# Short-rowed tiles in a pool of their own: every fp32r operand at a multiple of 256 bytes

## The chip, the cores and the metric

The kernel runs on one core of a Trainium2 chip. The metric is the time of one execution in microseconds (us), as the device counts it; times are compared as medians of several executions. The kernel before takes 1206.37 us (three runs, 1205.99 to 1206.79). A difference of about 0.2%, some 2.4 us, is the least that such a measurement tells from none.

## The reference

Two layers of a hybrid decoder trunk over 512 tokens of width 1024. Cut to what matters here:

```python
def hybrid_layer(x, c_silu, cos, sin, norm_g, w_ada, b_ada, w_in, sinks, w_br_a, w_br_b, w_br_c, w_out):
    mod = c_silu @ w_ada + b_ada
    shift, scale, gate = jnp.split(mod, 3, axis=-1)
    u = rms_norm(x, norm_g) * (1 + scale[:, None]) + shift[:, None]
    z = u @ w_in                     # (512 x 1024) @ (1024 x 8772)
    (aq, ak, av, ag, iq, ik, iw, bq, bk, bv, bg, cq, ck, cv, cg, ma, mb, mc) = jnp.split(z, SPLIT_OFFSETS, axis=-1)
    ya = dsa_attention(...)          # top-128 keys by an indexer, softmax
    yb = swa_sinks_attention(...)    # window of 128 keys, softmax with sinks
    yc = stick_breaking_attention(...)
    merged = (jax.nn.sigmoid(ma) * ((ya * silu(ag)) @ w_br_a)
              + jax.nn.sigmoid(mb) * ((yb * silu(bg)) @ w_br_b)
              + jax.nn.sigmoid(mc) * ((yc * silu(cg)) @ w_br_c))
    return x + gate[:, None] * (merged @ w_out)
```

All inputs and outputs are float32. The large products (u @ w_in, the three branch products, merged @ w_out) are most of the arithmetic.

## The kernel before

**Products in three parts.** TensorE multiplies float32 in a reduced form (fp32r) in one pass. To keep float32's accuracy, each operand of a large product is split into a high part and the rest: the weights into `whi` and `wlo`, the activations into `uh0` to `uh7` and `ul0` to `ul7` (one pair for each 128 features of u). A product is then the sum of three: hi by hi, hi by rest, rest by hi (`ttile`, and in the same way `branch_item` and `out_phase`). The gated mixer outputs, split, stand in `Y`; merged, split, stands in `vc` and `va` (high) and in `Q` and `KH` (rest).

**Tiling.** All activations lie transposed: 128 features on the partitions, the 512 tokens along the row. A tile of z is 128 columns by 512 tokens and is summed over eight blocks of 128 features, so it takes 24 products of a 128x128 block of weights (held in the array) with a 128x512 block of activations (streamed through it). A weight tile (`wstage`, then `whi` and `wlo`) holds four blocks of weights side by side, 512 floats or 2,048 bytes in a row; four such tiles of each are in use by turns. In the phase that makes the values (`v_phase`) it is the other way round: a block of `uh` is held and 364 columns of `whi` are streamed.

**Order.** The program is recorded first (`Recorder`), and a planner with a table of costs gives each instruction an engine and a place (`forward`, `order`); `emit` then writes each engine's instructions in that order. Nothing of this looks at where a tile lies in SBUF. The planner also picks the slot of a rotating tile (which of the four `whi`, which of the fourteen `t`).

**Where tiles lie.** Each partition of SBUF has one row of bytes. A pool lays its tiles one after another, in the order in which each is first asked for, each rounded up to a multiple of 32 bytes. Tiles of a fixed name come from the pool `const` (`fixed`, L589 and 590), the rotating ones from the pool `sb` (`Places.make`, L237 and 238), as the order of `emit` first reaches them (`Place.real`, L221 to 224). Rows of 2,048 or 4,096 bytes thus stand among rows of 4, 8, 16, 32, 64, 96 and 896 bytes, and each of those shifts all that follow it.

In the built program the tiles come to lie so, in bytes from the start of a partition, and by how much they exceed a multiple of 256:

| tile | first address before | over a multiple of 256 |
|---|---|---|
| `vc`, `va`, `Y` (five), `wstage` (four) | 36288, 44480, 52672, 60864 | 192 |
| `whi`, `wlo`: two slots of each | 93664, 97760 and 95712, 103904 | 224 |
| `whi`, `wlo`: the other two of each | 116224, 120320 and 118272, 124416 | 0 |
| `uh0`, `ul0` | 101856, 110048 | 224 |
| `uh1` to `uh7`, `ul1` to `ul7` | 122368 to 155136 | 0 |
| `Q` (both), `KI`, first `KH` | 185856, 183808, 177664 | 0 |
| second `KH` | 198848 | 192 |
| `klow0`, `klow1` | 22400, 25472 | 128 |
| `xm2` to `xm7` | 213376 to 223616 | 128 |

The blocks that a product takes out of a tile start at multiples of 256 bytes within it, so these numbers hold for the operands too. Of the program's fp32r products with a stream of 512 columns and all 128 rows there are 3,708:

| streamed operand | held operand | products |
|---|---|---|
| at a multiple of 256 | at a multiple of 256 | 1,333 |
| at a multiple of 256 | 224 over | 1,245 |
| 192 or 224 over | at a multiple of 256 | 536 |
| 192 or 224 over | 224 over | 594 |

The remaining fp32r products have streams of 128, 256, 364 or 384 columns, or take only half of the rows (the `pairs` of the low parts).

Of the kernel before, what the change touches and what calls it, by code (L numbers as in the profile page):

```python
# [25 lines left out]
F32 = mybir.dt.float32  # L26
F32R = mybir.dt.float32r
BF16 = mybir.dt.bfloat16
# [5 lines left out]
P = 128  # L34
# [116 lines left out]
         "m8": 2, "mx": 2, "nm": 2, "den": 2, "wstage": 4, "whi": 4, "wlo": 4, "ps_z": 3, "ps_s": 5}  # L151


class View:


# [73 lines left out]
class Places:  # L230
# [4 lines left out]
        self.tiles = []  # L235

    def make(self, shape, dtype, slot):  # L237
        return self.pool.tile(list(shape), dtype, name=self.name, tag=f"{self.name}_{slot}", bufs=1)


class Instr:
# [336 lines left out]
@with_exitstack  # L578
def trunk(ctx, tc, xT, vecs, w_ss, w_gt, w_first, w_t, w_v, w_br, w_o, rope, consts, out):
    nc = tc.nc  # L580
    const = ctx.enter_context(tc.tile_pool(name="const", bufs=1))
    sb = ctx.enter_context(tc.tile_pool(name="sb", bufs=1))
    ps = ctx.enter_context(tc.tile_pool(name="ps", bufs=1, space=bass.MemoryType.PSUM))
# [2 lines left out]
    rec = Recorder(tc, nc, ps, sb)  # L586
    PE, ACT, DVE, POOL, SP = (rec.engine(e) for e in ("PE", "ACT", "DVE", "POOL", "SP"))

    def fixed(name, shape, dt=F32):  # L589
        return rec.fixed(const.tile(shape, dt, name=name))  # L590

    def zbank():
        return rec.tile("ps_z", [P, S])
# [17 lines left out]
    f = lambda ap: ap.bitcast(F32)  # L611
# [25 lines left out]

    ACT.preload_act_table_set("natural_log_exp_and_others")
    small = fixed("small", [P, 16 + 40 * L + P], F32)
    SP.dma_start(small, vecs)  # L640
    csb, o = small[:, 0:8], 8
# [3 lines left out]
    sink, o = small[:, o:o + 8 * L], o + 8 * L  # L645
    ident = small[:, o:o + P]
    nones = fixed("nones", [P, P], F32R)
    DVE.memset(f(nones), -1.0)
    epst = fixed("epst", [P, 1], F32)
    DVE.memset(epst, EPS)  # L650
    cs = fixed("cs", [P, 8], F32)
# [957 lines left out]
```

## Time and profile before

| what | value |
|---|---|
| median of three runs | 1206.37 us |
| the profiled execution's own time | 1205.66 us |
| its span, first to last instruction | 1203.5 us |
| mean granted TensorE clock | 0.996 |
| ScalarE (ACT) busy | 565.8 us, 47% of the span |
| GpSimd (POOL) busy | 257.3 us, 21% |
| HBM read, written | 125.39 MB, 4.19 MB |

The profile names an engine's instructions by line, operation and tiles: "ps_z<-uh,whi" writes the PSUM tile ps_z from uh and whi. Nearly every instruction has the line of `emit` (L556, or L554 for pairs), so groups are told apart by their tiles. PE is TensorE's multiplications, PEld its loads of the held operand, DVE is VectorE. The duration that a multiplication has in the profile (some 395 ns at 512 columns) covers its way through the array, in which the next one has already begun; how fast they follow one another is read from their starts.

### The profile page before, as it was taken

The numbers are of one execution on the slowest core, as the hardware profiler recorded it, in microseconds if no ns is written. First come the engines' busy times: TensorE is split into PE (matmuls) and PEld (weight loads), VectorE is DVE, ScalarE is ACT, GpSimd is POOL, SyncE is SP. The second block draws the span as 40 slices with busy tenths as digits, with TensorE's granted clock in tenths as the row PEclk, the third lists the DMA queues.
The fourth block names the chain that finished last, engine by engine and source line by source line (L and its number), as shares of the span: only waits on it lengthen the run. The fifth ranks groups of instructions, "written<-read, shape, count | busy, mean of one in ns | idle before, by whom it ended". The sixth has DMA issues, their size and how long they took to land.

```text
span 1203.5 us, 17819 instructions
## 1 busy us (share of the span) xinstructions
PE 1181.2 (98%) x6006; PEld 969.7 (81%) x6006; DVE 958.3 (80%) x2094; ACT 565.8 (47%) x1177; POOL 257.3 (21%) x291
## 2 busy tenths in 40 slices
PE   9999999999999999999999999999999999999997
PEld 8799777788887887778898987777878778877886
DVE  6867999999888878786486699989897888667754
ACT  6533677564456532642143167665544654234222
POOL 1100355442010111001201016453221010111120
PEclk9999999999999999999999999999999999999999
DMA  9644323243434444344533433323342324323343
GB/s 318 229 121 123 91 71 89 87 123 114 122 100 129 132 141 140 88 129 148 165 112 98 136 95 81 86 71 115 115 123 79 97 80 123 96 66 84 94 123 99
DMA packets 81914, 139.39 MB, mean 116 GB/s; under 512 B 10016, under 2 KB 22560, under 8 KB 81824
## 3 DMA queue, kind: packets, MB, share of 16 engines
q1 hardware_dynamic: 80672, 136.17, 38.8%
q10 hardware_dynamic: 1152, 2.10, 0.5%
q8 instruction: 47, 0.77, 0.3%
q14 instruction: 43, 0.35, 0.1%
HBM read 125.39 MB, written 4.19 MB: 108 GB/s over the span
## 4 chain that ended last, share of the span: by engine, by line
PE 86%; DVE 6%; DMA 3%; ACT 2%; SPq 2%; issue 1%; POOL 0%; DVEq 0%; ACTq 0%
PE ps_z L556 67%; PE ps_s L556 14%; PE ps_s L554 5%; DMA wstage<-in_w_first 2%; DVE t L556 2%; SPq L556 2%; ACT t L556 1%; DVE KH L556 1%; DMA m<-zs 1%; DVE m L556 0%; DVE Y L556 0%; DVE zc L556 0%; DVE Q L556 0%; DVE wlo L556 0%; DMA wstage<-in_w_ss 0%
## 5 line engine op out<-in xcount | busy, mean ns | idle before, releaser
L556 PE MATMUL ps_z<-uh,whi 128*128 128x512 f32 (+1 forms) x908 | 360.1, 398 | 2.8 <-ACT e L556 1.2
L556 PE MATMUL ps_z<-uh,wlo 128*128 128x512 f32 (+1 forms) x908 | 357.0, 394 | 0.0
L556 PE MATMUL ps_z<-ul,whi 128*128 128x512 f32 (+1 forms) x908 | 356.0, 392 | 0.0
L556 POOL TENSOR_TENSOR wlo<-wstage,whi 128x512 fp32r<-128x512 f32 (+1 forms) x131 | 172.6, 1318 | 623.3 <-DVE whi L556 302.1
L556 PEld LDWEIGHTS ps_z<-uh,whi 128*128 128x128 f32 x908 | 170.6, 188 | 41.6 <-issue 2.1
L556 PEld LDWEIGHTS ps_z<-uh,wlo 128*128 128x128 f32 x908 | 171.0, 188 | 38.2 <-issue 1.7
L556 PEld LDWEIGHTS ps_z<-ul,whi 128*128 128x128 f32 x908 | 171.1, 188 | 34.6
L556 DVE TENSOR_TENSOR wlo<-wstage,whi 128x512 fp32r<-128x512 f32 (+2 forms) x241 | 159.0, 663 | 14.3 <-ACT whi L556 4.9
L556 ACT CAST whi<-wstage 128x512 fp32r<-128x512 f32 (+2 forms) x149 | 88.5, 597 | 169.1 <-PE ps_z L556 128.6
L556 DVE CAST whi<-wstage 128x512 fp32r<-128x512 f32 (+2 forms) x171 | 71.0, 416 | 112.9 <-PE ps_z L556 96.2
L556 PE MATMUL ps_z<-Y,whi 128*128 128x512 f32 x384 | 121.1, 396 | 1.1 <-ACT e L556 1.1
L556 ACT ACTIVATE e<-ps_z 128x512 f32<-128x512 f32 x68 | 40.3, 594 | 133.3 <-PE ps_z L556 133.0
L556 PEld LDWEIGHTS ps_z<-Y,whi 128*128 128x128 f32 x384 | 71.7, 188 | 18.3 <-issue 1.4
L556 ACT ACTIVATE e<-e 128x512 f32<-128x512 f32 x96 | 60.4, 631 | 37.3 <-DVE e L556 36.2
L556 ACT ACTIVATE t<-t 128x512 f32<-128x512 f32 x120 | 71.3, 627 | 13.2 <-DVE t L556 8.9
L556 POOL CAST whi<-wstage 128x512 fp32r<-128x512 f32 (+2 forms) x52 | 33.8, 651 | 200.8 <-PE ps_z L556 135.2
L556 PE MATMUL ps_z<-Y,wlo 128*128 128x512 f32 x192 | 75.7, 395 | 0.0
L556 ACT ACTIVATE t<-t,nm 128x256 f32<-128x256 f32 (+3 forms) x128 | 65.1, 510 | 17.3 <-DVE nm L556 17.1
L556 PE MATMUL ps_s<-small,t 128*128 128x128 f32 x432 | 59.1, 275 | 4.7 <-DVE t L556 4.4
L556 PEld LDWEIGHTS ps_s<-small,t 128*128 128x128 f32 x432 | 51.1, 142 | 14.2 <-issue 5.8
L556 DVE MAX8 m<-score 128x8 f32<-128x256 f32 (+2 forms) x96 | 53.5, 557 | 1.9
L556 PE MATMUL ps_s<-KH,Q 128*128 128x256 f32 (+3 forms) x280 | 52.0, 309 | 1.4 <-DVE t L556 1.4
(210 smaller groups left out, 2028.5 us busy)
## 6 DMA issues: line engine op xcount, KB each, us to landing
wstage<-in_w_t SPq DMA_DIRECT2D x212, 256.0 KB, 2.8
wstage<-in_w_v SPq DMA_DIRECT2D x48, 182.0 KB, 2.4
Y<-in_w_ss SPq DMA_DIRECT2D x16, 512.0 KB, 6.9
m<-zs SPq DMA_DIRECT2D x128, 64.0 KB, 2.0
wstage<-in_w_gt SPq DMA_DIRECT2D x32, 256.0 KB, 2.7
wstage<-in_w_ss SPq DMA_DIRECT2D x32, 256.0 KB, 2.8
wstage<-in_w_o SPq DMA_DIRECT2D x32, 256.0 KB, 2.8
wstage<-in_w_first SPq DMA_DIRECT2D x16, 256.0 KB, 4.0
```

The costliest lines, as they stand in the source:

```text
L554: self.real[engine].matmul(*[real(a) for a in q[:3]], start=q[3], stop=True, skip_group_check=True)
L556: getattr(self.real[engine], y.op)(*[real(a) for a in y.args], **{k: real(v) for k, v in y.kw.items()})
```

## The change

A function `pool_for` sends each tile whose row in bytes is no multiple of 256 to a new pool, `tiny`, that is laid out ahead of all others; it is used for the fixed tiles and for the rotating ones. One more tile, `gap` (128 bytes, never read or written), goes to that pool, so that it takes 1,920 bytes and ends at 18432, a multiple of 256. `const` and `sb` then begin at, and hold nothing but, multiples of 256.

```diff
+LINE = 256
+tiny = [None]
+
+
+def pool_for(pool, shape, dtype):
+
+    return pool if int(np.prod(shape[1:])) * (2 if dtype == BF16 else 4) % LINE == 0 else tiny[0]
+
...
     def make(self, shape, dtype, slot):
-        return self.pool.tile(list(shape), dtype, name=self.name, tag=f"{self.name}_{slot}", bufs=1)
+        return pool_for(self.pool, shape, dtype).tile(list(shape), dtype, name=self.name, tag=f"{self.name}_{slot}", bufs=1)
...
 def trunk(ctx, tc, xT, vecs, w_ss, w_gt, w_first, w_t, w_v, w_br, w_o, rope, consts, out):
     nc = tc.nc
+    tiny[0] = ctx.enter_context(tc.tile_pool(name="tiny", bufs=1))
     const = ctx.enter_context(tc.tile_pool(name="const", bufs=1))
...
     def fixed(name, shape, dt=F32):
-        return rec.fixed(const.tile(shape, dt, name=name))
+        return rec.fixed(pool_for(const, shape, dt).tile(shape, dt, name=name))
...
     DVE.memset(f(nones), -1.0)
+    fixed("gap", [P, 32], F32)
     epst = fixed("epst", [P, 1], F32)
```

No instruction is added, removed or moved: in the built program each engine's instructions stand in the order of before, with the same operands, the same slots and the same waits. Only addresses differ. Every tile of the first table lies at a multiple of 256 bytes, and so do all operands of all 5,028 fp32r products; `Y` starts at 53248, the `whi` at 94208, 98304, 116736 and 120832, `uh0` at 102400, `uh1` at 122880. In `tiny` lie the vectors of one to 24 floats, `small` and the 32-byte scratch of the top-k and the softmaxes. `small`, at 16512, has not moved. The last tile ends 128 bytes further on than before.

## Prediction

> **What bounds the kernel now.** First the page's head, its row by slices for the clock, and the chain of waits.
>
> ```profile
> span 1203.5 us, 17819 instructions
> PE 1181.2 (98%) x6006; PEld 969.7 (81%) x6006; DVE 958.3 (80%) x2094; ACT 565.8 (47%) x1177; POOL 257.3 (21%) x291
> PEclk9999999999999999999999999999999999999999
> PE 86%; DVE 6%; DMA 3%; ACT 2%; SPq 2%; issue 1%; POOL 0%; DVEq 0%; ACTq 0%
> PE ps_z L556 67%; PE ps_s L556 14%; PE ps_s L554 5%; DMA wstage<-in_w_first 2%; DVE t L556 2%; SPq L556 2%; ACT t L556 1%; DVE KH L556 1%; DMA m<-zs 1%; DVE m L556 0%; DVE Y L556 0%; DVE zc L556 0%; DVE Q L556 0%; DVE wlo L556 0%; DMA wstage<-in_w_ss 0%
> ```
>
> TensorE multiplies during 98% of the span at its full clock, and of the chain that ended last 86% is TensorE, 67% of the span in ps_z alone. So the kernel is as fast as its products follow one another. Next, what these products are: the groups of instructions with their shapes kept apart.
>
> ```profile
> L556 PE MATMUL ps_z<-uh,whi 128*128 128x512 f32 x884 | 353.3, 401 | 2.7 <-ACT e L556 1.2 <-DVE xm L556 0.9 <-ACT uh L556 0.7
> L556 PE MATMUL ps_z<-uh,wlo 128*128 128x512 f32 x884 | 350.0, 396 | 0.0
> L556 PE MATMUL ps_z<-ul,whi 128*128 128x512 f32 x884 | 349.4, 395 | 0.0
> L556 PE MATMUL ps_z<-Y,whi 128*128 128x512 f32 x384 | 121.1, 396 | 1.1 <-ACT e L556 1.1
> L556 PE MATMUL ps_z<-Y,wlo 128*128 128x512 f32 x192 | 75.7, 395 | 0.0
> ...
> L556 PE MATMUL ps_z<-Q,whi 128*128 128x512 f32 x48 | 19.0, 397 | 0.0
> ```
>
> With the five other groups of 48 (streams from vc, va and KH), 3,516 products of 512 columns go to ps_z; 192 more go to ps_s, 3,708 in all. Their durations overlap, so what counts is the step from one start to the next. The kernel before already contains both kinds of operands, and one engine runs them within microseconds of each other. The timeline of PE, start and duration in us:
>
> ```profile
> 408.08 0.39 PE L556 MATMUL ps_z<-uh,whi 128*128 128x512 f32 x1
> ...
> 410.12 0.39 PE L556 MATMUL ps_z<-uh,whi 128*128 128x512 f32 x1
> ...
> 410.80 0.39 PE L556 MATMUL ps_z<-uh,whi 128*128 128x512 f32 x1
> ...
> 412.85 0.39 PE L556 MATMUL ps_z<-uh,whi 128*128 128x512 f32 x1
> ...
> 413.55 0.39 PE L556 MATMUL ps_z<-uh,whi 128*128 128x512 f32 x1
> ...
> 418.44 0.40 PE L556 MATMUL ps_z<-uh,whi 128*128 128x512 f32 x1
> ...
> 419.14 0.40 PE L556 MATMUL ps_z<-uh,whi 128*128 128x512 f32 x1
> ...
> 423.91 0.63 PE L556 MATMUL ps_z<-Y,whi 128*128 128x512 f32 x2
> ...
> 432.22 0.63 PE L556 MATMUL ps_z<-Y,whi 128*128 128x512 f32 x2
> ...
> 435.02 0.39 PE L556 MATMUL ps_z<-uh,whi 128*128 128x512 f32 x1
> ```
>
> The addresses of the built program say what each stretch is. From 408.08 to 412.85 come 21 products, the blocks 1 to 7 of one tile of z, streams and held weights all at multiples of 256: 4.77 us, **227.1 ns a step**. From 413.55 to 418.44 come 21 again, the same streams, but from weight slots 224 over: 4.89 us, **232.9 ns**. From 419.14 to 423.91, with aligned slots, it is 4.77 us once more. From 432.22 to 435.02, 12 products stream Y, 192 over, with aligned weights: 2.80 us, **233.3 ns**. Same engine, shape and clock; only the addresses differ, and one unaligned operand of either kind is enough.
>
> **The change, part by part.** Products of 512 columns: 2,375 of the 3,708 have an unaligned operand (1,245 + 536 + 594, from the program), and all of them become aligned. A step falls from 233.0 to 227.1 ns, between 232.9 − 227.1 = 5.8 and 233.3 − 227.1 = 6.2; I take 6.0. 2,375 × 6.0 ns = **14.3 us** less of TensorE. Starts are shown to 0.01 us, 0.5 to 0.8 ns in such a step, so the bounds are 5.3 and 6.7 ns, 12.6 and 15.9 us.
>
> [...]
>
> Shorter products: the value phase streams 364 columns.
>
> ```profile
> 81.41 0.33 PE L556 MATMUL ps_s<-whi,uh 128*128 128x364 f32 x1
> ...
> 85.41 0.33 PE L556 MATMUL ps_s<-whi,uh 128*128 128x364 f32 x1
> ...
> 89.41 0.33 PE L556 MATMUL ps_s<-whi,uh 128*128 128x364 f32 x1
> ```
>
> 24 products from aligned slots of whi and wlo (81.41 to 85.41) take 4.00 us, and 24 from slots 224 over (85.41 to 89.41) take 4.00 us, 166.7 ns each. So I count nothing for the 576 of these, and nothing for the other short shapes; the bound above is 6 ns for each of the 1,320 fp32r products outside the 3,708, 7.9 us, far from this row and therefore a rival.
>
> The other engines: four casts and six subtractions of the weight split on DVE, over both kinds of slots, in one stretch:
>
> ```profile
> L556 DVE TENSOR_TENSOR wlo<-wstage,whi x6: 679/691/693, 405.8 to 422.5; 128x512 fp32r<-128x512 f32 x6
> L556 DVE CAST whi<-wstage x4: 420/424/427, 409.9 to 418.9; 128x512 fp32r<-128x512 f32 x4
> ```
>
> Minimum, median and maximum lie within 14 ns, without a second kind. DVE, and ACT and POOL by likeness, get 0. Loads: those into wstage (192 over) and those into G (a multiple of 256 today) stand at
>
> ```profile
> wstage<-in_w_o SPq DMA_DIRECT2D x32, 256.0 KB, 2.8
> G<-xsave SPq DMA_DIRECT2D x8, 256.0 KB, 2.7
> ```
>
> 0.1 us of 2.8 is 4%. The chain holds 3% DMA, 36 us, mostly at the start: at most 1.3 us gained, and 0 taken. The pool `tiny` gathers scratch of DVE, ACT and POOL in 1.9 KB; no row shows such neighbours disturbing each other, and I take 0 between −0.5 and +0.5 us.
>
> How much reaches the end: ps_z on the chain is 67% of 1203.5, 806 us. The 3,516 products at the mean step of (2,375 × 233.0 + 1,333 × 227.1) ÷ 3,708 = 230.9 ns are 812 us, and ps_z has some 55 us of shorter ones, so 806 ÷ 867 = 93% of them lie on the chain. 14.3 × 0.93 = **13.3 us**. The rest runs while TensorE waits anyway, mostly for DVE:
>
> ```profile
> PE ps_s L556 <- DVE t L556: 5.8, 4, 3.0
> PE ps_z L556 <- ACT e L556: 2.3, 2, 1.2
> ```
>
> Then what is late next. DVE is the engine closest behind: the sum of the windows 150 to 300 and 700 to 900 us, and the tightest of them (columns: window, length, busy time and instructions of PE, PEld, DVE, ACT, POOL, clock, DMA):
>
> ```profile
> 200.00:250.00 50.00, 48.29 (x250) 37.44 (x250) 47.99 (x103) 33.02 (x70) 25.32 (x28) 1.00 0.32 96
> ...
> sum 350.00, PE 344.81 PEld 273.24 DVE 326.60 ACT 212.47 POOL 147.10; mean PE 49.26 PEld 39.03 DVE 46.66 ACT 30.35 POOL 21.01
> ```
>
> DVE is busy 93% of these 350 us (stick-breaking, top-k and rotary work beside the products). They are 29% of the span and, at an even density, hold 14.3 × 0.29 = 4.1 us of the gain. DVE's 23.4 us of idle time would allow all of it, but its order is fixed and TensorE waits for it there, so some turns into longer waits: between 0 and 4.1 us; I take a third, 1.4, nearer to 0 since DVE still has over five times that idle. 13.3 − 1.4 = **11.9 us**. From the profiled execution's 1205.66 that is 1193.8; the median of before lies 0.7 us higher, at 1206.37, which gives 1194.5. I forecast **1194 us**, 1.0% less. Ends: 15.9 us all on the chain gives 1190.5, 12.6 × 0.8 − 4.1 = 6.0 us gives 1200.4.
>
> **The rivals.**
>
> 1. *DVE becomes the bound.* If TensorE's waits for DVE absorb all of the gain in the dense stretches and half of it elsewhere, 13.3 − 4.1 − 4.6 = 4.6 us stay: about 1202 us. For it: 93% busy, and waits for its t that are there already. Against: outside these windows DVE has idle time, and 86% of the chain is TensorE.
> 2. *The change does nothing.* If the step depends on something that goes along with the address (which slot was loaded when, say), or TensorE has no address term: 1206 us. For it: the 364-column rows show none. Against: the same 6 ns with Y and aligned weights, and within one tile of z. [...]
> 3. *Slower: operands meet in the same place.* Afterwards streams, held weights and the split's outputs nearly all start at multiples of 2,048 bytes. If reads that begin at equal places disturb each other by as much as misalignment costs now, the 1,333 aligned products get 6 ns longer and the others stay: +8.0 us, 1214 us. It decides if equal offsets cost more than nothing; today's rows are against it, since from 410.12 to 410.80 (0.68 us, 3 products, 227 ns) stream and held block of uh4 and whi lie exactly 18,432 bytes, nine times 2,048, apart. Only three-way meetings are untried.
> 4. *More than forecast.* If the short products gain too, up to 7.9 us, or the loads' 1.3 us, the time is 1185 to 1190 us.
>
> **How the numbers follow.** The forecast case (1190.5 to 1200.4) has 0.76: both steps of its main term are measured in this trace. Rival 1 has 0.10, rival 2 0.06, rival 3 0.04, rival 4 0.04. The range 1190 to 1201 holds the forecast case and the near end of rival 1, about 8 in 10. Faster by over 0.2% (about what a measurement of this kernel can tell from no change) are the forecast and rivals 1 and 4, 0.90; within it rival 2, 0.06; slower rival 3, 0.04.
>
> **What would show it.** In the profile after, the uh products of every tile of z should step at 227 ns, those from Y too, and none of the stretches at 233 should be left; the 364-column steps should stay at 166.7. PE's busy time should fall by about as much as the span, and its waits for DVE grow by 1 to 3 us. If steps are 227 and the span has fallen by less than 6 us, the conversion failed (rival 1), to be seen in the waits and in windows 150 to 300. If steps of 233 or more remain in the same number, it is rival 2 or 3.

## The result, and the profile after

The changed kernel takes **1194.02 us** (median of four runs, 1190.49 to 1195.28), the kernel before beside it on the same chip 1206.18 (four runs, 1205.76 to 1206.79). The ratio is 0.9894, with a 95% interval of 0.9872 to 0.9916: 1.1% faster, where 1194 was forecast. The profiled execution took 1194.35 us. Beside the later runs the kernel before spread from 1201.48 to 1207.32 us, and medians of it from 1204.72 to 1206.18, so a few runs tell less than the 0.2% that was set out above.

The head of the page and the chain of waits, after:

```profile
span 1192.2 us, 17819 instructions
PE 1167.9 (98%) x6006; PEld 968.8 (81%) x6006; DVE 961.0 (81%) x2094; ACT 565.3 (47%) x1177; POOL 256.4 (22%) x291
PE 85%; DVE 8%; ACT 2%; DMA 2%; SPq 2%; issue 1%; DVEq 0%; POOL 0%; ACTq 0%
PE ps_z L565 65%; PE ps_s L565 15%; PE ps_s L563 5%; DVE t L565 3%; SPq L565 2%; ACT t L565 1%; DVE m L565 1%; DVE KH L565 1%; DMA wstage<-in_w_first 1%; DMA m<-zs 1%; DVE Q L565 0%; DVE zc L565 0%; DMA rt<-in_rope 0%; DVE wstage L565 0%; DVE score L565 0%
```

TensorE's busy time fell by 13.3 us (from 1181.2), the span by 11.3 (from 1203.5). DVE's share of the chain grew from 6% to 8%. The groups, shapes apart:

```profile
L565 PE MATMUL ps_z<-uh,whi 128*128 128x512 f32 x884 | 350.7, 398 | 2.2 <-ACT e L565 1.2 <-DVE xm L565 1.0
L565 PE MATMUL ps_z<-uh,wlo 128*128 128x512 f32 x884 | 347.3, 393 | 0.0
L565 PE MATMUL ps_z<-ul,whi 128*128 128x512 f32 x884 | 346.8, 392 | 0.6 <-DVE ul L565 0.6
L565 PE MATMUL ps_z<-Y,whi 128*128 128x512 f32 x384 | 118.8, 390 | 1.1 <-ACT e L565 1.1
```

Each is 2.3 to 2.7 us less busy than before. That understates the gain, since durations overlap (some 390 ns each, starts 227 ns apart); the steps show it. The timeline of PE in the part where the prediction compared the tiles:

```profile
405.66 0.40 PE L565 MATMUL ps_z<-uh,whi 128*128 128x512 f32 x1
...
421.32 0.62 PE L565 MATMUL ps_z<-Y,whi 128*128 128x512 f32 x2
...
424.04 0.39 PE L565 MATMUL ps_z<-uh,whi 128*128 128x512 f32 x1
```

69 products of uh and ul take 15.66 us, 227.0 ns a step, through all four slots of the weights; the 12 of Y take 2.72 us, 226.7 ns, where the kernel before needed 233.3.

The program order is the same, so the two timelines can be joined product by product. Steps over 250 ns (a wait, or half the clock, 430 ns a step) left out:

| products of 512 columns, by their addresses before | joined | fall of a step, ns | sum, us |
|---|---|---|---|
| only the held block off 256 | 1,201 | 5.5 | 6.6 |
| only the stream off | 513 | 6.0 | 3.1 |
| both off, by different amounts | 390 | 5.8 | 2.3 |
| both off by the same 224 bytes | 164 | 3.0 | 0.5 |
| both at multiples of 256 | 1,277 | 1.3 | 1.7 |
| together | 3,545 | | 14.1 |

The other shapes: steps of 364 columns did not change, those of 256 columns (520) got 1 ns *longer*, 0.7 us in all. From the first multiplication to the last the time fell by 10.96 us, so by balance all the rest, waits and the like, took 14.1 − 0.7 − 10.96 = 2.4 us more. That balance belongs to this pair of traces and not to the change: in the trace of after_again, the same changed kernel run once more (below), the products give 14.2 us, and first to last is 15.85 us shorter than in the kernel before, so there the rest took 2.3 us *less*.

PE's waits (sum, times, longest), and DVE in the dense windows (the tightest, and the sum of 150 to 300 and 700 to 900):

```profile
PE ps_s L565 <- DVE t L565: 7.1, 7, 3.1
PE ps_z L565 <- ACT e L565: 2.3, 2, 1.2
...
PE ps_s L565 <- ACT t L565: 1.5, 2, 1.4
```

```profile
200.00:250.00 50.00, 47.83 (x246) 37.30 (x246) 48.33 (x103) 32.16 (x70) 25.34 (x28) 1.00 0.34 101
...
sum 350.00, PE 343.87 PEld 274.81 DVE 328.54 ACT 210.93 POOL 146.16; mean PE 49.12 PEld 39.26 DVE 46.93 ACT 30.13 POOL 20.88
```

The wait for DVE's t grew from 5.8 to 7.1 us, and DVE is busy 2 us more of the same 350, which now hold slightly more of the program. The loads beside the products hardly moved: wstage<-in_w_o lands in 2.7 us (2.8 before).

### The profile page after: what moved, and what is told of

Same layout as the page of the kernel before. It is cut to its first block, busy times and chain, and to the rows that moved or that the text cites. A ratio compares the mean times of both kernels' runs of the same rounds, so it can differ in the third digit from the quotient of the medians.

```text
span 1192.2 us, 17819 instructions
## 1 busy us (share of the span) xinstructions
PE 1167.9 (98%) x6006; PEld 968.8 (81%) x6006; DVE 961.0 (81%) x2094; ACT 565.3 (47%) x1177; POOL 256.4 (22%) x291
## 4 chain that ended last, share of the span: by engine, by line
PE 85%; DVE 8%; ACT 2%; DMA 2%; SPq 2%; issue 1%; DVEq 0%; POOL 0%; ACTq 0%
PE ps_z L565 65%; PE ps_s L565 15%; PE ps_s L563 5%; DVE t L565 3%; SPq L565 2%; ACT t L565 1%; DVE m L565 1%; DVE KH L565 1%; DMA wstage<-in_w_first 1%; DMA m<-zs 1%; DVE Q L565 0%; DVE zc L565 0%; DMA rt<-in_rope 0%; DVE wstage L565 0%; DVE score L565 0%
## 5 line engine op out<-in xcount | busy, mean ns | idle before, releaser
L565 DVE TENSOR_TENSOR wlo<-wstage,whi 128x512 fp32r<-128x512 f32 (+2 forms) x241 | 158.0, 659 | 12.2 <-ACT whi L565 3.7
L565 ACT ACTIVATE t<-t 128x512 f32<-128x512 f32 x120 | 71.7, 628 | 12.6 <-DVE t L565 8.9
L565 DVE SCALAR_TENSOR_TENSOR wstage<-wstage,csr 128x512 f32<-128x512 f32 x64 | 49.4, 774 | 6.0 <-DMA wstage<-in_w_ss 3.2
```

Source lines behind the costliest of these rows:

```text
L565: getattr(self.real[engine], y.op)(*[real(a) for a in y.args], **{k: real(v) for k, v in y.kw.items()})
```

## The experiments

**Place or distance?** The prediction took it that each operand by itself has to begin at a multiple of 256 bytes (theory 1, place). The rival: what counts is how far apart the stream and the held block lie, modulo 256 (distance). The 198 products above with both operands 224 over (164 of them joined) already lean to it. A kernel of products alone settles it: groups of 24, each with its own pair of offsets.

```python
for i in range(count):
    a = i % 3 * 1024 + s // es      # stream, s bytes over
    b = i % 6 * 128 + w_ // es      # held block, w_ bytes over
    nc.tensor.matmul(p[:, :n], st[kind][:, b:b + 128], mv[kind][:, a:a + n], ...)
```

> The step alone: groups of 24 products that follow one another (12 for float32), streams and held blocks moved by 0 to 256 bytes each, 512 down to 128 columns, in fp32r, bf16 and float32. All of the reference's computation is left out. Theory 1 (both operands of an fp32r product must begin at a multiple of 256 bytes): 227 ns a step at 512 columns where both offsets are 0 or 256, 233 ns at all others, however small the offset, and no difference at 364 columns and below. Rival (a smaller unit, 64 or 128 bytes, is enough): 227 ns also at offsets of 64 or 128. Rival (the distance between the two operands counts, not their place): 227 ns wherever both are moved by the same amount. Rival (the address does not matter at all, it only went along with the slots): one step for all.

Its timeline of PE. A name is type (zr fp32r, zb bf16), columns (A 512, F 256), and the offsets of stream and held block (a 0, b 32, c 64, e 128, f 160, g 192, h 224, k 256 bytes); a group's time is the difference of two starts.

```profile
119.78 5.76 PE L62 MATMUL zrA_ae<-mvr,str 128*128 128x512 f32 x24
125.38 5.76 PE L62 MATMUL zrA_af<-mvr,str 128*128 128x512 f32 x24
130.99 5.67 PE L62 MATMUL zrA_ag<-mvr,str 128*128 128x512 f32 x24
136.49 5.76 PE L62 MATMUL zrA_ah<-mvr,str 128*128 128x512 f32 x24
142.09 5.61 PE L62 MATMUL zrA_ak<-mvr,str 128*128 128x512 f32 x24
147.53 5.64 PE L62 MATMUL zrA_bb<-mvr,str 128*128 128x512 f32 x24
153.01 5.64 PE L62 MATMUL zrA_cc<-mvr,str 128*128 128x512 f32 x24
...
163.96 5.64 PE L62 MATMUL zrA_ee<-mvr,str 128*128 128x512 f32 x24
169.43 5.64 PE L62 MATMUL zrA_ff<-mvr,str 128*128 128x512 f32 x24
```

Only the held block moved by 128 (ae): 5.60 us ÷ 24 = 233.3 ns. By 256 (ak): 5.44 us, 226.7 ns. *Both* moved, by 32 (bb) or by 128 (ee): 5.48 and 5.47 us, 228 ns. Both operands off 256 and yet nearly the short step: **the distance counts, and theory 1 is wrong.** What is left for the place is 1.4 ns at most (226.7 against 228). One other distance costs less than the rest: the stream 64 bytes past the held block, modulo 256 (ag, 0 against 192, is such a one: 5.50 us, 229 ns). By this rule the 198 products that lay 224 over, both of them, should have gained about 1 ns; they gained 3.0, and the difference is not explained.

256 columns of fp32r, and bf16, from the same timeline:

```profile
302.29 3.02 PE L62 MATMUL zrF_aa<-mvr,str 128*128 128x256 f32 x24
305.15 3.00 PE L62 MATMUL zrF_ba<-mvr,str 128*128 128x256 f32 x24
307.98 3.00 PE L62 MATMUL zrF_ea<-mvr,str 128*128 128x256 f32 x24
...
346.05 5.34 PE L62 MATMUL zbA_ba<-mvb,stb 128*128 128x512 bf16 x24
351.23 5.34 PE L62 MATMUL zbA_ea<-mvb,stb 128*128 128x512 bf16 x23
```

bf16 takes 5.18 us ÷ 24 = 215.8 ns at every distance that was tried (0, 32 and 128 bytes). Groups of 12 plain float32 products, two records each, take 10.30 us at every distance, 858 ns a product, where one of fp32r is a single record and steps at some 230 ns. At 256 columns of fp32r, distance 0 takes 2.86 us, 119.2 ns, and 32 bytes 2.83 us, 117.9: the order is reversed, and the kernel's 256-column steps, which got longer by 0.7 us in all, went the same way.

**The same in the kernel.** Without the tile `gap`, all 5,028 products have both operands 128 over: place off, distance 0. With `gap` three times as long, everything lies 256 further on.

```diff
-    fixed("gap", [P, 32], F32)      # no_gap
```

```diff
-    fixed("gap", [P, 32], F32)      # gap_256
+    fixed("gap", [P, 96], F32)
```

> The changed kernel without the tile gap: const and sb begin 128 bytes earlier, so all 5,028 fp32r products have both operands 128 over a multiple of 256, at the same distances from one another as in the change. Theory 1: all 3,708 steps of 512 columns cost 6 ns more, 22 us of TensorE, of which 80 to 95% reach the end: 1212 to 1215 us, slower than even the kernel before. Rival (multiples of 128 are enough) and rival (only the distance counts, or the order of the pools): 1194 us.

> The changed kernel with a gap of 384 bytes for 128: everything behind the pool tiny lies 256 bytes further on, at odd multiples of 256. Theory 1: no change, 1194 us, within 2 us. Rival (the gain comes from starts at multiples of 512 or 2,048): 1212 to 1215 us. Rival 3 of the prediction (equal places modulo 2,048 cost something): unchanged too, since all move alike.

no_gap: 1194.33 us (1194.04 to 1195.51), ratio to before 0.991 (0.9894 to 0.9927), the time of the changed kernel. gap_256: 1192.13 us (1189.46 to 1194.16), 0.9891 (0.9873 to 0.991). Its products of 512 columns sum to within 0.2 us of the changed kernel's, so it does not matter at which multiple of 256 the tiles begin. All tiles moved alike here, so this run leaves their distances open; those are tried further below. PE's timeline in no_gap:

```profile
408.20 0.39 PE L565 MATMUL ps_z<-uh,whi 128*128 128x512 f32 x1
...
421.12 0.39 PE L565 MATMUL ps_z<-uh,whi 128*128 128x512 f32 x1
```

57 products in 12.92 us are 226.7 ns a step, with not one operand at a multiple of 256. The tile `gap` does nothing; what the change does is to keep the short rows out from between the long ones.

**Distance put back.** `whi` and `wlo` alone are moved, by 128 bytes in one kernel and by 192 (a distance of 64) in the other; 3,660 products then lie that far from their streams.

```diff
-        return pool_for(self.pool, shape, dtype).tile(...)
+        pool = split[0] if self.name in ("whi", "wlo") else pool_for(self.pool, shape, dtype)
+        return pool.tile(...)
...
+    split[0] = ctx.enter_context(tc.tile_pool(name="split", bufs=1))
+    split[0].tile([P, 32], F32, name="ahead")     # weights_192: [P, 48]
+    rest = ctx.enter_context(tc.tile_pool(name="rest", bufs=1))
+    rest.tile([P, 32], F32, name="behind")        # weights_192: [P, 16]
```

> The changed kernel with whi and wlo alone moved 128 bytes on, in a pool of their own; all else stays at multiples of 256. 3,660 of the 3,708 products then have streams at 0 and held blocks at 128. Theory 2 (what counts is the distance between the stream and the held block, modulo 256): 233.5 ns a step as in the isolated groups, 23 to 24 us more TensorE, of which 80 to 95% reach the end: 1212 to 1217 us. Rival (multiples of 128 are enough, which also explains the run without the gap): 1194 us.

> As weights_128, but whi and wlo 192 bytes on, so that the stream lies 64 bytes behind a multiple of 256 from the held block. In the isolated groups this distance cost 228.7 (stream moved by 64) and 229.4 ns (held block moved by 192). Theory 2 with these steps: 2.0 to 2.7 ns for each of 3,660 products, 7 to 10 us, 80 to 95% of it at the end: 1199 to 1204 us. Rival (every distance but 0 costs the same): 1212 to 1217 us.

weights_128: 1208.0 us (ten runs, 1204.05 to 1209.99), ratio 1.0024 (1.001 to 1.0038): the whole gain is gone and a little more. weights_192: 1198.06 us (1194.48 to 1200.42), ratio 0.9938 (0.9922 to 0.9954). The two timelines of PE, weights_128 first:

```profile
407.85 0.39 PE L567 MATMUL ps_z<-uh,whi 128*128 128x512 f32 x1
...
423.19 0.40 PE L567 MATMUL ps_z<-uh,whi 128*128 128x512 f32 x1
```

```profile
404.59 0.39 PE L567 MATMUL ps_z<-uh,whi 128*128 128x512 f32 x1
...
419.70 0.39 PE L567 MATMUL ps_z<-uh,whi 128*128 128x512 f32 x1
```

66 products each: 15.34 us, 232.4 ns, and 15.11 us, 228.9 ns. Both kernels came out faster than was expected of them: the step at 128 bytes is 232.5 ns in the mean of the kernel, not 233.5, so the products take 18.2 us longer than in the changed kernel. Against the kernel before on its own chip (1204.72 and 1206.18 us) weights_128 is 3.3 us slower and the changed kernel 12.2 faster, so some 15.4 of the 18.2 us reached the end. PE's wait for t is 2.8 us in its trace, against 7.1 in the changed kernel's; that this is where the rest went was not tested.

**Which block does the stream meet?** While a block streams, the next one is being loaded (the changed kernel's loads, PEld, are busy 968.8 us of a span of 1192.2 in which PE is busy 1167.9), so "the held block" could be a product's own or the next one's. Pairs of products alternate by 128 bytes so that only one of the two pairings is at distance 0. Other groups try 464 to 504 columns.

```python
("own",  ss=(0, 128), ws=(0, 128))    # stream of product i meets its own block at 0
("next", ss=(128, 0), ws=(0, 128))    # it meets the block of product i + 1 at 0
("both", ss=(0, 0),   ws=(0, 0)),  ("none", ss=(128, 128), ws=(0, 0))
```

> The step alone once more, fp32r, 48 products a group; all of the reference's computation is left out. Groups one: stream and held block at fixed places, 0 to 2,048 bytes apart. Groups own and next: places alternate between 0 and 128 bytes over, so that a stream lies like the block that it is multiplied with (own) or like the block that is loaded while it runs, the next one (next); own_s and next_s the same with 64 bytes. Theory 2a (the stream's reads meet those of the load of the next block): 227 ns in next, 233 in own. Theory 2b (stream and its own block): 227 in own, 233 in next. Neither counts alone: both between. Groups one: 227 at 0 and at every multiple of 256, 229 at 64, 232 to 234 elsewhere; a step that differs between 256 and 2,048 would show a larger unit. Columns: 504 to 464 show between 512 (6 ns) and 448 (1 to 4 ns) how the cost of 128 bytes fades.

Its timeline of PE, groups of 48 (onen is a fixed distance of 2,048 bytes; nC is 480 columns, a at distance 0, e at 128; nD 464):

```profile
152.62 11.04 PE L60 MATMUL zonen<-mvr,str 128*128 128x512 f32 x48
163.50 11.14 PE L60 MATMUL zown<-mvr,str 128*128 128x512 f32 x48
174.48 11.20 PE L60 MATMUL znext<-mvr,str 128*128 128x512 f32 x48
185.52 11.06 PE L60 MATMUL zboth<-mvr,str 128*128 128x512 f32 x48
196.42 11.35 PE L60 MATMUL znone<-mvr,str 128*128 128x512 f32 x48
207.61 11.28 PE L60 MATMUL zown_s<-mvr,str 128*128 128x512 f32 x48
...
273.51 10.57 PE L60 MATMUL znCa<-mvr,str 128*128 128x480 f32 x48
283.92 10.40 PE L60 MATMUL znCe<-mvr,str 128*128 128x480 f32 x48
294.16 10.19 PE L60 MATMUL znDa<-mvr,str 128*128 128x464 f32 x48
```

both 227.1, own 228.8, next 230.0, none 233.1 ns: neither pairing explains it alone, so both theories of this run fell; each counts in part. In the kernel before, the 1,277 products whose own operands lay right still gained 1.3 ns, 1.7 us in all. About 0.9 us of it is from 201 of them with a neighbour that lay wrong: 69 whose stream lay off the next product's block gained 6.6 ns each, and 128 that followed a product with a stream off its own block gained 3.6. The other 0.8 us is from 1,038 whose neighbours on both sides lay right too; they gained 0.7 ns each, and why is open. Nor do the two pairings weigh alike in kernel and groups: at the borders between stretches of the kernel before, 80 products whose stream lay right to the next block alone stepped at 229.0 ns, and 73 with their own block alone right at 233.7, the other way round from next (230.0) and own (228.8). Distances of 512, 1,024 and 2,048 bytes gave 226.7 ns each, as 256 did. At 480 columns the distance of 128 is the *faster* one, 213.3 against 216.9 ns. What in the chip makes these steps is open.

**Does DVE keep part of the gain?** The top-k of the indexer is a large part of DVE's work in the dense stretches. It is taken out of the kernel before (notopk_b) and of the changed one (notopk_a).

```diff
-            for n in range(TOPK // 8):
-                def fn(i=i):
-                    s = st["score", i]
-                    m8 = m8_tile()
-                    DVE.max(m8, s)
-                    DVE.match_replace(s, m8, s, LOW)
-                yield op(0, fn)
-                yield wait(SPACE["t"])
```

> The kernel before without the 96 pairs of MAX8 and MATCH_REPLACE8 of the top-k, some 100 us of VectorE in its dense stretches; the indexer's scores go to their threshold unsorted, and the planner orders the rest anew. Only its difference to the next run counts. If VectorE keeps part of the gain from the end, the pair without top-k differs by 13 us or more, near the 14 us that the steps give; if not, by 11 to 12 us as the pair with top-k does. The kernel itself: 1195 to 1206 us.

> The changed kernel with the same part of the top-k left out; its order of instructions is that of the run before it, only the addresses differ. 13 to 14.5 us faster than it if VectorE kept part of the gain, 11 to 12 us if something else did.

1198.74 us (1197.98 to 1201.22) and 1186.14 us (1184.96 to 1187.72): the change brings 12.6 us by medians, where it brought 12.2 with the top-k. In the joined timelines of this pair the products again give 14.1 us, and waits and the rest take 0.6 more, where the first pair had 2.4 more and the trace of after_again 2.3 less. So single traces cannot say it, and the medians do not tell 12.6 from 12.2: **inconclusive**.

**The longest wait.** In layer 2 TensorE waits 3.11 us for t, at 796.73 us in the changed kernel (2.98 in the kernel before). DVE is then at three subtractions of the indexer's rest part, with a scan of the stick-breaking behind them in its queue. DVE's timeline of the changed kernel:

```profile
791.09 4.25 DVE L565 TENSOR_TENSOR KH<-zc,KH 64x512 fp32r<-64x512 f32 x3
795.37 1.22 DVE L565 TENSOR_TENSOR_SCAN t<-ps_s,t 128x511 f32<-128x511 f32 x1
796.50 0.67 DVE L565 SCALAR_TENSOR_TENSOR t<-ps_s,t 128x512 f32<-128x512 f32 x1
```

In kh_before and kh_after the three stand behind the scan and the instruction after it, in both layers; after_again is the changed kernel, unedited.

```diff
-    rec.emit(rec.order())
+    rec.emit(kh_later(rec.order()))      # puts KH<-zc,KH x3 two DVE instructions later
```

> The kernel before, with three DVE subtractions of the indexer's rest part (KH<-zc,KH, 4.25 us together) moved behind the scan and the subtraction of stick-breaking that follow them, in both layers; addresses as before. If the 3.0 us wait of TensorE for t in layer 2 is due to these three instructions, it shrinks below 2 us and the granted clock stays at 1.00 there (the stretch 790 to 815 us has 0.91 in the kernel before): 1.2 to 3 us of wait and 1.7 us of half clock go, 1200.5 to 1203 us. Rival: the queue of DVE is only shuffled and something else of it is late (KH itself, or the next scan): a wait of the same sum at another place, 1204 to 1207.

> The same move in the changed kernel. With the clock at 1.00 in both, this against kh_before is the change without the chance of the half clock. By the first theory 1189 to 1192 us, 11 to 13 us less than kh_before, and the single times lie closer together than those of the changed kernel (1190.5 to 1195.3); by the rival 1193 to 1196.

> The changed kernel again, beside the two others on the same chip: 1190 to 1196 us, with the granted clock below 1.00 between 790 and 815 us wherever its wait for t there is about 3 us.

kh_before: 1202.93 us (1201.38 to 1205.18), ratio 0.9985 (0.9975 to 0.9996). **kh_after: 1188.18 us** (1186.52 to 1191.91), ratio 0.9865 (0.9843 to 0.9887). after_again: 1192.24 us (1189.46 to 1195.54), ratio 0.9897 (0.9876 to 0.9918). kh_after is the fastest by medians, just under the 1189 to 1192 that were expected; its interval still overlaps that of after_again, so its 0.3% over the changed kernel is likely and not certain. With the wait cut in both, the change is worth 1202.93 − 1188.18 = 14.8 us (11 to 13 were expected), against 1204.98 − 1192.24 = 12.7 with it, on the same chip. So what the change's gain lost on its way to the end may have been lost at this wait; with medians that scatter by some 2 us either way it is a lean, not a proof. The times of kh_after do not lie closer together than those of the changed kernel, as the first theory had it; and its account of the clock fell, which the last section shows.

## Why the prediction was right, step by step

- **The bound** held: TensorE is 85% of the chain (86% before), and the time follows its steps.
- **The main term**, 2,375 × 6.0 = 14.3 us, measured 14.1 for all joined products of 512 columns. That the sizes agree is in part luck, for the reason given was wrong. "One unaligned operand of either kind is enough" read place into rows that showed distance: in every stretch that was quoted an unaligned operand met an aligned one, and the kernel before had 198 products with both 224 over, which were counted at 6.0 ns. They gave 3.0. Those counted at nothing, the 1,333 with aligned operands, gave 1.7 us. The two errors have opposite signs and nearly cancel: what the prediction's mechanism has left when it is put as distance is 2,177 products at 5.67 ns, 12.3 us. By place no_gap would have been slower than before; it is as fast as the changed kernel.
- **Short products**: the 364-column steps stayed at 166.7 ns, as taken. Those of 256 columns were put at nothing by likeness and cost 0.7 us.
- **Other engines and loads** at 0: the loads beside the products land in 2.7 us instead of 2.8, ACT and POOL are within 1 us of their busy times before, DVE is busy 2.7 us longer (961.0 against 958.3).
- **From the sum to the end**: 93% on the chain and 1.4 us kept by DVE, 11.9 of 14.3 us. By medians 12.2 of 14.1 arrived, 12.7 in the repeat. The share is about right. The wait for t grew from 5.8 to 7.1 us in the first trace and to 6.7 in after_again's, within the "1 to 3 us" of waits that were forecast or just short of them; that DVE kept the rest of the gain is not shown. The traces of two executions of the changed kernel differ by 4.8 us in waits and rest, with the same steps, which is more than the 1.4 us in question. So the forecast's agreement to a fraction of a microsecond is luck; the repeat's median is 1192.24.
- **Rival 1** (DVE becomes the bound, 1202) did not come. **Rival 2** fell with the steps of 227 ns. **Rival 3**, the slower one (equal places modulo 2,048), is the opposite of what the runs show: equal distances are the fast case, 226.7 ns at 2,048 bytes. **Rival 4** did not come: the short products lost a little.

## What to carry to other kernels

For fp32r products of 512 columns, look at the address of the stream minus that of the held block: a multiple of 256 bytes saved 6 ns of 233 here, and rows of a few bytes laid out between long ones were what broke it. Aligning everything is one way to get there; bf16 (215.8 ns), plain float32 (858) and, in the kernel, 364 columns (166.7) gain nothing; in the isolated groups 504 columns gain 6 ns and 464 2, and 256 and 480 columns lose 1 to 4 ns. So the width of the stream has to be tried, too. Before a cost is put down to an operand's own place, one pair with *both* operands moved alike should be timed.

## What the runs showed of the hardware

The steps above were not expected: 227 to 228 ns where stream and held block lie a multiple of 256 bytes apart, 229 where the stream is 64 bytes past that and 233 to 234 at other multiples of 32, for 512 columns of fp32r. The first group of each of the two kernels of products alone stands outside of this, at distance 0 right behind the warm-up: 235.8 and 231.5 ns. In steps2 the same engine with the same blocks takes 227.1 ns (both) or 233.1 (none) by nothing but how its two operands lie to each other.

The second surprise is the clock. After its wait of 3.11 us the changed kernel ran some products at half speed. The timeline of PE:

```profile
796.73 0.41 PE L565 MATMUL ps_s<-small,t 128*128 128x128 f32 x2 [3.11 <-DVE t L565]
...
798.20 0.63 PE L565 MATMUL ps_z<-ul,whi 128*128 128x512 f32 x1
798.63 0.63 PE L565 MATMUL ps_z<-uh,wlo 128*128 128x512 f32 x1
```

From 798.20 to 798.63 one product took 0.43 us, almost twice 0.227. The granted clock is 0.50 from 798.00 to 801.41 us, 3.41 us, which costs about 1.7. But the length of the wait alone does not decide it. The rows of 790 to 815 us (the granted clock is the third number from the end; the kernel before has 0.93 there, not the 0.91 that the expectation of kh_before names) in the changed kernel, in after_again and in kh_before, one after the other:

```profile
790.00:815.00 25.00, 21.89 (x113) 16.85 (x112) 22.54 (x39) 13.03 (x24) 13.26 (x17) 0.93 0.30 85
```

```profile
790.00:815.00 25.00, 21.68 (x116) 16.42 (x114) 23.93 (x54) 12.01 (x24) 12.56 (x13) 1.00 0.28 87
```

```profile
790.00:815.00 25.00, 22.25 (x109) 16.60 (x108) 22.97 (x36) 14.19 (x26) 13.45 (x18) 0.93 0.20 61
```

after_again waited 3.04 us, and its clock stayed at 1.00:

```profile
793.33 0.41 PE L565 MATMUL ps_s<-small,t 128*128 128x128 f32 x2 [3.04 <-DVE t L565]
```

kh_before waited 0.77 and then 1.98 us, and its clock was halved:

```profile
799.43 0.66 PE L556 MATMUL ps_s<-small,t 128*128 128x128 f32 x4 [0.77 <-ACT t L556]
...
802.76 0.33 PE L556 MATMUL ps_s<-small,t 128*128 128x128 f32 x1 [1.98 <-DVE t L556]
```

So a wait of 3.04 us went without a half clock, and one followed a wait of 1.98 with a short burst ahead of it.

The traces' clock records give the lengths. In the kernel before, whose wait of 2.98 us ended at 802.49 us, the clock is at 0.50 from 802.33 to 805.74 us, 3.41 us as in the changed kernel. The first stretch at full clock lasts 795.31 us in the kernel before and 791.89 in the changed one, the next 392.53 and 385.71: 233, 232, 115 and 113 times 3.4133 us, a common step that is an estimate from these four lengths. In the 3.41 us just ahead of the half clock TensorE was idle for 2.14 us in the changed kernel (794.59 to 798.00) and for 2.81 in the kernel before (798.91 to 802.33). In kh_before the half clock began at some 803.6 us, and the wait of 1.98 us had ended 0.8 us earlier. What starts a half clock, and why the 3.04 us of after_again went without one, is not shown.

A stretch of half clock costs 1.7 us, a part of the 5 to 6 us by which executions of one kernel differ, and a reason not to read the difference of two single traces as that of two kernels.
